# Whole fp32 query products for three of four slices, and the masks of a chunk inverse on VectorE

## The chip, the cores and the metric

The kernel runs on one core of a Trainium2 chip. The core has TensorE (PE in the profile, with its weight loads as PEld), VectorE (DVE), ScalarE (ACT), GpSimd (POOL) and the queue of SyncE (SP), and 16 DMA engines. The metric is the device time of one execution in microseconds (us); of several runs the median is given.

## The reference

One layer of a trunk over 1024 tokens of width 1024. A combined projection feeds an RWKV-7 branch (a recurrence over tokens in 8 heads of 64) and a latent attention with a block-causal mask; both are gated and added. Then comes a retrieval layer over 16,384 experts of one neuron each, then a small gated embedding and a last norm. What bears on this case:

```python
    state = state * w_t + sa[..., None] * b_t + v_t[..., None] * k_t      # RWKV-7, token by token
    ...
    def one_block(xb):                                                    # retrieval, 128 tokens
        q = (xb @ w_q).reshape(t, PEER_HEADS, 2, HALF_Q)
        s = jnp.einsum('thcd,hcnd->thcn', q, sub_keys).astype(jnp.float32)
        top_s, top_i = lax.top_k(s, PEER_TOPK)
        cand_s = (top_s[:, :, 0, :, None] + top_s[:, :, 1, None, :]).reshape(...)
        best_s, best_pos = lax.top_k(cand_s, PEER_TOPK)
        idx = jnp.take_along_axis(cand_i, best_pos, axis=-1)              # 8 heads x 16 per token
        gate = jax.nn.softmax(best_s, axis=-1)
        act = jax.nn.gelu(jnp.einsum('td,thkd->thk', xb, u_tab[idx]), approximate=False)
        return jnp.einsum('thk,thkd->td', gate * act, v_tab[idx])
```

Every token picks 128 experts. Their rows of table u (4 KB each) are multiplied with the token's activation, and their rows of table v are summed with the weights that come out.

## The kernel before, in words

The 1024 tokens are eight blocks of 128, taken two at a time as four slices (0 to 3). For each slice the kernel runs `project_rwkv` and `project_rest` (the combined projection), `rwkv` (the recurrence, in chunks of 64 tokens), `attend`, and `select`.

`rwkv` prepares chunks in `chunk_pre`: products within a chunk come to a tile `gs` (L612), and the inverse of a triangular matrix is built in six levels. At each level a mask takes one band out of `gs`: two multiplications of 128x256 into the tile `lm` (L621), which has two buffers. TensorE multiplies `lm` with the running inverse `x` (L586), and VectorE adds the product to `x` and `xt` (L642, L645). There are eight `chunk_pre`, two per slice, so 96 mask multiplications. They are made by `self.aux`, which is GpSimd while `rwkv` is written out and VectorE otherwise. GpSimd makes the token differences (L497) and three more small steps of `rwkv` too.

`select` joins the branches, projects them (L785), normalises, transposes the activation (`to_T`), and makes the queries: 16 tiles of weights `w_q`, 8 products of 128x128 by 128x256 each. Before the change every product is split: an fp32 number is written as a high part (a cast to fp32r by ScalarE, L280) and a low part (the remainder by a subtraction, L282, on GpSimd for these weights; L261 on VectorE for the activation), and high times high, high times low and low times high are summed (L292, L293, L294). The other projections take whole fp32 products (L290). The query is multiplied with the keys (L813), and VectorE finds the top 16 of each (L824 to L828). `combine` makes the 128 indices per token (up to the cast at L869).

`gather` then fetches, for each block, 128 times 128 rows of u by an indirect DMA from GpSimd's queue (L900) and has VectorE take the dot with the activation (L902). The rows land in four buffers in turn, seven from the dense product on. For blocks 0 to 4 the weighted sum over v is not gathered: `expand` spreads the weights into a dense matrix (L959, L961) which is written to memory, and `dense` multiplies it with all of v in split products (L280, L282, L996 to L998) and adds the sums (L1001). For blocks 5 to 7 the rows of v are gathered (L915) and added one by one (L917). `ple` does the last step of each block.

The order of the work is made when the kernel is built: each stage is written with a priority (a low number goes first; `gather` has a high one), and a scheduler places every instruction on its engine by these priorities and a timeline of its own. On the chip each engine takes its queue strictly in that order. So a gather on GpSimd waits behind whatever stands ahead of it in GpSimd's queue, and a dot that lacks its row holds up all that follows on VectorE.

Of the kernel before, what the change touches and what calls it, by code (L numbers as in the profile page):

```python
# [9 lines left out]
R = mybir.dt.float32r  # L10
# [141 lines left out]
class Program:  # L152
# [131 lines left out]
    def mm(self, ps, w, a, k, start=True, stop=True):  # L284

        mm = self.nc.tensor.matmul
        for i in range(k):
            first, last = start and i == 0, stop and i == k - 1
            if len(w) == 1:
                mm(ps, w[0][:, i], a[0][:, i], start=first, stop=last)  # L290
            else:
                mm(ps, w[0][:, i], a[0][:, i], start=first, stop=False)  # L292
                mm(ps, w[0][:, i], a[1][:, i], start=False, stop=False)  # L293
                mm(ps, w[1][:, i], a[0][:, i], start=False, stop=last)  # L294
# [293 lines left out]
    def chunk_pre(self, pool, psum, B):  # L588


        nc = self.nc
        t = lambda shape, tag, bufs=2: self.tile(pool, shape, F, tag, bufs)
        bank = lambda shape: self.tile(psum, shape, F, "inv", 2)
        ar, kb, v = B["ar"], B["kb"], B["v"]
        eye = self.c("eye2")
        mm = nc.tensor.matmul
        halves = (slice(0, 64), slice(64, 128))
        G, V = [], []
        for c in range(2):
            gs = t([128, 4, 2, 192], "gs", 3)  # L600
            vs = t([128, 4, 64], "vs", 3)
            ts = slice(c * 64, c * 64 + 64)
            for j in range(4):
                ps = bank([128, 448])
                for a in range(2):
                    for p in halves:
                        mm(ps[p, a * 192:a * 192 + 128], kb[p, a, j, ts], ar[p, j, c], start=True, stop=True)
                    for p in halves:
                        mm(ps[p, a * 192 + 128:a * 192 + 192], kb[p, a, j, ts], eye[p], start=True, stop=True)
                for p in halves:  # L610
                    mm(ps[p, 384:448], v[p, j, ts], eye[p], start=True, stop=True)
                nc.vector.tensor_tensor(gs[:, j], ps[:, :384].rearrange("p (a n) -> p a n", a=2),  # L612
                                        self.c("gmask")[:, None, :].to_broadcast([128, 2, 192]), op=OP.mult)
                nc.scalar.activation(vs[:, j], ps[:, 384:448], AF.Copy)
            G.append(gs)
            V.append(vs)

        def level(l):
            m = t([128, 8, 64], "lm", 2)
            for c in range(2):  # L620
                self.aux.tensor_tensor(m[:, 4 * c:4 * c + 4], G[c][:, :, 0, 0:64],  # L621
                                       self.c("lmask")[:, None, l * 64:l * 64 + 64].to_broadcast([128, 4, 64]), op=OP.mult)
            return m

        eye_b = eye[:, None, :].to_broadcast([128, 8, 64])
        lm = level(0)
        z = bank([128, 8, 64])
        self.each(z, (lambda j: lm[:, j], lambda j: eye))
        x = t([128, 8, 64], "x", 1)
        nc.vector.tensor_tensor(x, z, eye_b, op=OP.add)  # L630
        xt = t([128, 8, 64], "xt", 2)
        nc.vector.tensor_tensor(xt, lm, eye_b, op=OP.add)
        for l in range(1, 6):
            lm = level(l)
            z = bank([128, 8, 64])
            self.each(z, (lambda j: lm[:, j], lambda j: x[:, j]))
            zs = t([128, 8, 64], "zs", 1)
            nc.scalar.activation(zs, z, AF.Copy)
            if l < 5:
                d = bank([128, 8, 64])  # L640
                self.each(d, (lambda j: xt[:, j], lambda j: zs[:, j]))
                nc.vector.tensor_tensor(x, x, d, op=OP.add)  # L642
            d = bank([128, 8, 64])
            self.each(d, (lambda j: zs[:, j], lambda j: xt[:, j]))
            nc.vector.tensor_tensor(xt, xt, d, op=OP.add)  # L645
        return G, V, xt
# [106 lines left out]
    def select(self, hf, side="left"):  # L753
        nc = self.nc
        bl = SLICES[hf]
        NB, N = len(bl), len(bl) * 128
        ts = self.tile(self.kp, [128, NB, 8, 2, 16], F, "ts", 1)
        ti = self.tile(self.kp, [128, NB, 8, 2, 16], U32, "ti", 1)
        with ExitStack() as s2:
            pool = self.pool(s2, "se", side)  # L760
            psum = self.pool(s2, "sp", side, True)
            t, bank = self.makers(pool, psum)
# [4 lines left out]
            m = t([128, 8, N], "act")  # L767
            for d in range(8):
                ys = []
                for i, src in enumerate(("rw_wo", "mla_wo")):  # L770
                    w = self.weights(self.wp, self.I[src][d], 4)
# [8 lines left out]
            for k in range(8):  # L780
                w = self.tile(self.wp, [128, 8, 128], F, "w", WBUF).rearrange("p a n -> p (a n)")
# [14 lines left out]
            for b, x in zip(bl, xs):  # L796
                nc.vector.scalar_tensor_tensor(x, x, rs[:, b - bl[0]:b - bl[0] + 1], gf, op0=OP.mult, op1=OP.mult)
                nc.sync.dma_start(self.h2[b], x)
            hT = [t([128, 8, N], "act", 2, R) for _ in range(2)]
            self.to_T(bank, xs, hT)  # L800
            for i in range(16):
                raw, = self.weights(self.wp, self.I["w_q"][i], 8)
                w = [t([128, 8, 128], n, 1, R) for n in (("whi", "wlo") if i % 2 == 0 else ("x0", "x1"))]
                self.split_to(w, raw, nc.gpsimd)
                ps = bank([128, N])
                self.mm(ps, w, hT, 8)
                q = t([128, N], "gate", 4)
                nc.scalar.activation(q, ps, AF.Copy)
                keys = t([128, 128], "keys", 3)
                nc.sync.dma_start(keys, self.I["keys"][:, i])  # L810
                ps = bank([128, NB, 128], "tr", 1)
                for b in range(NB):
                    nc.tensor.matmul(ps[:, b], q[:, b * 128:b * 128 + 128], keys, start=True, stop=True)  # L813
                s = t([128, NB, 128], "s", 5)
                nc.scalar.activation(s, ps, AF.Copy)
                for b in range(NB):
                    self.top16(s[:, b], ts[:, b, i // 2, i % 2], ti[:, b, i // 2, i % 2])
# [303 lines left out]
```

## Time and profile before

| | |
|---|---|
| median of 3 runs | 3949.66 us (3947.78 to 3959.03) |
| the profiled execution | 3942.72 us, its span 3940.7 us |
| granted TensorE clock, mean | 0.880 |
| VectorE busy | 3193.8 us, 81% |
| TensorE busy | 3087.6 us, 78% |
| GpSimd busy | 2050.4 us, 52% |
| ScalarE busy | 1276.9 us, 32% |
| DMA | 1160.48 MB, mean 294 GB/s |

The page gives one execution. A row of instructions names the line, the engine, the operation, what it writes and reads, its shape and count, then its busy time and the mean of one, and behind the second bar how long the engine was idle before it and on whom it waited. The chain of waits follows the work that ended last back from the end; "issue" in it is time in which an engine waited for nothing that the profile shows. A stretch is given by its start and end in us from the span's start.

### The profile page before, as it was taken

Reading aid. Unit: us, or ns where it says so; the run is one execution under the profiler, and the core shown is the slowest. Engines: PE = TensorE matmul, PEld = TensorE weight load, DVE = VectorE, ACT = ScalarE, POOL = GpSimd, SP = SyncE. Lnnn points to the kernel's source line nnn. Section 1 sums busy time; section 2 is a strip of 40 time slices with the busy share of each in tenths; the row PEclk is TensorE's granted clock in tenths of the full one; section 3 lists DMA queues with packets and bytes.
Section 4 is the critical chain, followed back from the end, with each engine's and each line's share of the span. In section 5 each row is a group of like instructions: output and inputs, shape, how many; then the busy total and the mean of one; then the engine's idle time right before and its main releaser. Section 6 shows DMA issues by size and latency. Waiting matters only on the chain.

```text
span 3940.7 us, 62191 instructions
## 1 busy us (share of the span) xinstructions
PE 3087.6 (78%) x21999; PEld 2517.8 (64%) x21999; DVE 3193.8 (81%) x6931; ACT 1276.9 (32%) x2723; POOL 2050.4 (52%) x1638
## 2 busy tenths in 40 slices
PE   7998778678879794878866687568888889989581
PEld 7885767666668673578735567446666667767351
DVE  2532888767899685899878778998999999999997
ACT  3231222133222174222138867522221222222341
POOL 0201456645654533576454425446767776666754
PEclk9998899888989796888967788779999999999796
DMA  6236598899868998878888998799999999999986
GB/s 200 88 112 200 183 321 286 285 318 309 313 188 309 322 323 285 305 243 279 311 276 284 302 336 274 233 321 341 386 384 371 390 379 372 373 385 352 329 279 232
DMA packets 502327, 1160.48 MB, mean 294 GB/s; under 512 B 54016, under 2 KB 228352, under 8 KB 502016
## 3 DMA queue, kind: packets, MB, share of 16 engines
q0 software_dynamic: 202752, 738.29, 52.7%
q1 hardware_dynamic: 281984, 402.48, 30.3%
q10 hardware_dynamic: 17280, 15.74, 1.2%
q8 instruction: 174, 2.85, 0.3%
q14 instruction: 137, 1.12, 0.1%
HBM read 1071.38 MB, written 84.93 MB: 293 GB/s over the span
## 4 chain that ended last, share of the span: by engine, by line
DVE 23%; PE 23%; issue 20%; DMA 17%; POOL 10%; ACT 5%; SPq 2%; POOLq 0%; DVEq 0%; ACTq 0%
DVE u L902 9%; DMA u<-in_u_dram,idx 9%; PE mm L290 7%; POOL u L900 6%; POOL u L915 4%; PE mm L785 2%; DVE oa L959 2%; PE w L961 1%; PE inv L586 1%; PE acc L997 1%; DMA u<-in_v_dram,idx 1%; DMA raw<-zT 1%; PE acc L998 1%; PE mm L292 1%; SPq L964 1%
## 5 line engine op out<-in xcount | busy, mean ns | idle before, releaser
L900 POOL DMA_INDIRECT u<-in_u_dram,idx x1024 | 1230.5, 1202 | 1182.1 <-DVE dots L902 625.2
L902 DVE CUSTOM_DVE_ANT_0 u<-u,gh 128x1024 f32<-128x1024 f32 x1024 | 1320.8, 1303 | 226.8 <-DMA u<-in_u_dram,idx 210.1
L915 POOL DMA_INDIRECT u<-in_v_dram,idx x384 | 485.7, 1265 | 230.6 <-DVE x L917 104.1
L290 PE MATMUL mm<-hT,w 128*128 128x128 f32 x4608 | 568.4, 284 | 11.8 <-DMA raw<-zT 3.5
L997 PE MATMUL acc<-vlo,Whi 128*128 128x512 f32 x1280 | 521.8, 408 | 67.4 <-DVE vlo L282 66.8
L290 PEld LDWEIGHTS mm<-hT,w 128*128 128x128 f32 x4608 | 553.1, 199 | 27.6 <-ACT z L326 7.8
L998 PE MATMUL acc<-vhi,Wlo 128*128 128x512 f32 x1280 | 513.4, 401 | 0.0
L996 PE MATMUL acc<-vhi,Whi 128*128 128x512 f32 x1280 | 374.3, 402 | 101.8 <-ACT vhi L280 83.0
L996 PEld LDWEIGHTS acc<-vhi,Whi 128*128 128x128 f32 x1280 | 244.9, 193 | 176.5 <-ACT vhi L280 93.1
L997 PEld LDWEIGHTS acc<-vlo,Whi 128*128 128x128 f32 x1280 | 248.4, 194 | 147.1 <-DVE vlo L282 96.7
L917 DVE SCALAR_TENSOR_TENSOR x<-u,gate,x 128x1024 f32<-128x1024 f32 x256 | 329.2, 1286 | 6.0 <-DMA u<-in_v_dram,idx 2.1
L280 ACT ACTIVATE vhi<-vr 128x512 fp32r<-128x512 f32 x256 | 158.8, 628 | 532.2 <-DMA vr<-in_v_dram 347.6
L961 PE MATMUL w<-ob,oa 128*128 128x128 f32 x1280 | 225.3, 334 | 98.1 <-ACT ob L955 53.5
L961 PEld LDWEIGHTS w<-ob,oa 128*128 128x128 f32 x1280 | 203.6, 240 | 124.9 <-ACT ob L955 81.6
L998 PEld LDWEIGHTS acc<-vhi,Wlo 128*128 128x128 f32 x1280 | 249.1, 195 | 51.6
L959 DVE TENSOR_SCALAR oa<-cst,pt 128x128 f32<-128x128 f32 x640 | 210.7, 388 | 39.3 <-PE w L961 34.8
L954 ACT ACTIVATE ob<-cst,pt 128x128 f32<-128x128 f32 x640 | 204.3, 396 | 0.6 <-PE w L961 0.5
L282 DVE TENSOR_TENSOR vlo<-vr,vhi 128x512 fp32r<-128x512 f32 x256 | 174.7, 693 | 8.0 <-ACT vhi L280 7.9
L280 ACT ACTIVATE Whi<-wr 128x1280 fp32r<-128x1280 f32 x64 | 81.5, 1273 | 287.0 <-PE acc L997 257.6
L917 DVE SCALAR_TENSOR_TENSOR gh<-u,gate,gh 128x1024 f32<-128x1024 f32 x128 | 167.9, 1311 | 4.9 <-DMA u<-in_v_dram,idx 3.0
L290 PE MATMUL mm<-act,w 128*128 128x256 f32 x512 | 134.0, 417 | 45.2 <-DMA act<-yg 29.1
L621 POOL TENSOR_TENSOR lm<-gs,cst 128x256 f32<-128x256 f32 x96 | 100.1, 1063 | 100.9 <-DVE gs L612 56.6
(331 smaller groups left out, 5511.6 us busy)
## 6 DMA issues: line engine op xcount, KB each, us to landing
w<-in_w_in_dram SPq DMA_DIRECT2D x144, 512.0 KB
vr<-in_v_dram SPq DMA_DIRECT2D x256, 256.0 KB
W<-ws SPq DMA_DIRECT2D x40, 1024.0 KB
wr<-W SPq DMA_DIRECT2D x64, 640.0 KB
w<-in_w_q_dram SPq DMA_DIRECT2D x64, 512.0 KB
w<-in_w_out_dram SPq DMA_DIRECT2D x32, 512.0 KB
u<-in_u_dram,idx POOLq DMA_INDIRECT x1024, 6.9
x<-in_x_dram SPq DMA_DIRECT2D x16, 512.0 KB
```

The costliest lines, as they stand in the source:

```text
L280: self.nc.scalar.activation(act[0], x, AF.Copy)
L290: mm(ps, w[0][:, i], a[0][:, i], start=first, stop=last)
L900: nc.gpsimd.indirect_dma_start(out=u[:], out_offset=None, in_=self.I["u"], in_offset=bass.IndirectOffsetOnAxis(ap=idx[:, k:k + 1], axis=0))
L902: nc.vector.tensor_tensor_reduce(out=u[:], in0=u[:], in1=h[:], scale=1.0, scalar=0.0, op0=OP.mult, op1=OP.add, accum_out=dots[:, k:k + 1])
L915: nc.gpsimd.indirect_dma_start(out=v[:], out_offset=None, in_=self.I["v"], in_offset=bass.IndirectOffsetOnAxis(ap=idx[:, k:k + 1], axis=0))
L917: nc.vector.scalar_tensor_tensor(x, v, gate[:, k:k + 1], x, op0=OP.mult, op1=OP.add)
L954: nc.scalar.activation(c[:, i], self.c("iota"), AF.Abs, bias=pt[:, 1, k + i:k + i + 1])
L959: nc.vector.tensor_scalar(a, self.c("iota"), pt[:, 0, k:k + 1], pt[:, 2, k:k + 1], op0=OP.is_equal, op1=OP.mult)
L961: nc.tensor.matmul(ps[:, i], a, c[:, i], start=True, stop=True)
L996: nc.tensor.matmul(acc[b], wh, vh, start=i == 0, stop=False)
L997: nc.tensor.matmul(acc[b], wh, vl, start=False, stop=False)
L998: nc.tensor.matmul(acc[b], wl, vh, start=False, stop=i == G - 1)
```

## The change

The masks of `chunk_pre` are made by VectorE. In `select`, slice 0 keeps the split queries; slices 1 to 3 transpose the activation into one fp32 tile and multiply it with the weights as they were loaded, so that the casts, the subtractions and the split tiles of the weights, and the low part of the activation, are not made.

```diff
@@ chunk_pre, level(l)
             for c in range(2):
-                self.aux.tensor_tensor(m[:, 4 * c:4 * c + 4], G[c][:, :, 0, 0:64],
+                nc.vector.tensor_tensor(m[:, 4 * c:4 * c + 4], G[c][:, :, 0, 0:64],
                                        self.c("lmask")[:, None, l * 64:l * 64 + 64].to_broadcast([128, 4, 64]), op=OP.mult)
@@ select
-            hT = [t([128, 8, N], "act", 2, R) for _ in range(2)]
+
+            split = hf == 0
+            hT = [t([128, 8, N], "act", 2, R) for _ in range(2)] if split else [t([128, 8, N], "act")]
             self.to_T(bank, xs, hT)
             for i in range(16):
                 raw, = self.weights(self.wp, self.I["w_q"][i], 8)
-                w = [t([128, 8, 128], n, 1, R) for n in (("whi", "wlo") if i % 2 == 0 else ("x0", "x1"))]
-                self.split_to(w, raw, nc.gpsimd)
+                w = (raw,)
+                if split:
+                    w = [t([128, 8, 128], n, 1, R) for n in (("whi", "wlo") if i % 2 == 0 else ("x0", "x1"))]
+                    self.split_to(w, raw, nc.gpsimd)
                 ps = bank([128, N])
                 self.mm(ps, w, hT, 8)
```

The scheduler makes a new order from it. Lines behind L805 stand four further down in the changed kernel. GpSimd's queue among the queries of slice 1, before (`u` is a buffer of a gathered row, `wlo` and `x` are low parts of the weights), and then the same gathers in the changed order:

```order
L900 DMA u_1255_5233<-in_u_dram,idx_1010_4457 128x1024
L282 TENSOR_TENSOR wlo_9023<-w_9020,whi_9022 128x1024
L282 TENSOR_TENSOR x_1946_9073<-w_9070,x_1945_9072 128x1024
L900 DMA u_5236<-in_u_dram,idx_1010_4457 128x1024
L900 DMA u_5239<-in_u_dram,idx_1010_4457 128x1024
L900 DMA u_5242<-in_u_dram,idx_1010_4457 128x1024
L282 TENSOR_TENSOR wlo_9123<-w_9120,whi_9122 128x1024
L900 DMA u_1259_5245<-in_u_dram,idx_1010_4457 128x1024
L282 TENSOR_TENSOR x_1962_9173<-w_9170,x_1961_9172 128x1024
L900 DMA u_5248<-in_u_dram,idx_1010_4457 128x1024
```

```order
L904 DMA u_1255_5233<-in_u_dram,idx_1010_4457 128x1024
L904 DMA u_5236<-in_u_dram,idx_1010_4457 128x1024
L904 DMA u_5239<-in_u_dram,idx_1010_4457 128x1024
L904 DMA u_5242<-in_u_dram,idx_1010_4457 128x1024
L904 DMA u_1259_5245<-in_u_dram,idx_1010_4457 128x1024
L904 DMA u_5248<-in_u_dram,idx_1010_4457 128x1024
```

The splits between the gathers are gone; in the rows before, one to three gathers stood between two of them. VectorE's queue at the first levels of an inverse of slice 1, before and then changed (`krt`, `lst`, `ms` are small tiles of norms):

```order
L218 SCALAR_TENSOR_TENSOR krt_6307<-kry_6306 8x128
L630 TENSOR_TENSOR x_5969<-inv_5952,cst_60 128x512
L902 ISA u_4697,dots_4534<-u_4697,gh_4532 128x1024
L902 ISA dots_4534 128x1
L390 TENSOR_SCALAR ms_7543<-sum_7385 128x256
L902 ISA u_1077_4700,dots_4534<-u_1077_4700,gh_4532 128x1024
L902 ISA dots_4534 128x1
```

```order
L218 SCALAR_TENSOR_TENSOR krt_6307<-kry_6306 8x128
L630 TENSOR_TENSOR x_5969<-inv_5952,cst_60 128x512
L906 ISA u_1077_4700,dots_4534<-u_1077_4700,gh_4532 128x1024
L906 ISA dots_4534 128x1
L621 TENSOR_TENSOR lm_6031<-gs_5841,cst_60 128x256
L621 TENSOR_TENSOR lm_6031<-gs_5895,cst_60 128x256
L906 ISA u_4703,dots_4534<-u_4703,gh_4532 128x1024
L906 ISA dots_4534 128x1
```

Each level's two masks now stand among the dots, here behind one that reads a gathered row. The last place is VectorE's queue at the end of the dense product: its last sums into the blocks' rows (`x` from `acc`), before and then changed.

```order
L917 SCALAR_TENSOR_TENSOR x_6608_30642<-u_30983,gate_4131_20116,x_6608_30642 128x1024
L1001 TENSOR_TENSOR x_5354_24164<-x_5354_24164,acc_6450_30076 128x512
L1001 TENSOR_TENSOR x_5355_24166<-x_5355_24166,acc_6451_30077 128x512
L1001 TENSOR_TENSOR x_5356_24168<-x_5356_24168,acc_6452_30078 128x512
L1001 TENSOR_TENSOR x_5357_24170<-x_5357_24170,acc_6453_30079 128x512
L917 SCALAR_TENSOR_TENSOR x_6608_30642<-u_30986,gate_4131_20116,x_6608_30642 128x1024
L1001 TENSOR_TENSOR x_5358_24172<-x_5358_24172,acc_6454_30080 128x512
```

```order
L921 SCALAR_TENSOR_TENSOR gh_30041<-u_6672_30142,gate_4047_19230,gh_30041 128x1024
L1005 TENSOR_TENSOR x_5255_23177<-x_5255_23177,acc_6351_29089 128x512
L1005 TENSOR_TENSOR x_5256_23179<-x_5256_23179,acc_6352_29090 128x512
L921 SCALAR_TENSOR_TENSOR gh_30041<-u_30145,gate_4047_19230,gh_30041 128x1024
L1005 TENSOR_TENSOR x_5257_23181<-x_5257_23181,acc_6353_29091 128x512
L1005 TENSOR_TENSOR x_5258_23183<-x_5258_23183,acc_6354_29092 128x512
L1005 TENSOR_TENSOR x_5259_23185<-x_5259_23185,acc_6355_29093 128x512
```

Before, the additions of v rows have come to block 6 (`x_6608`) when the dense product ends: 243 additions stand ahead. Changed, they have come to block 7, whose rows are summed in `gh`: 291 stand ahead. Likewise 731 dots stand ahead of the dense product's first low part of v (`vlo`, L282) before, and 768, all of blocks 0 to 5, in the changed order.

## The prediction

> **What bounds the kernel now.** I read the page's busy shares first, then the engines by stretches of the run.
>
> ```profile
> PE 3087.6 (78%) x21999; PEld 2517.8 (64%) x21999; DVE 3193.8 (81%) x6931; ACT 1276.9 (32%) x2723; POOL 2050.4 (52%) x1638
> 0.00:480.00 480.00, 410.05 (x4111) 356.81 (x4112) 200.84 (x733) 134.27 (x298) 79.64 (x67) 0.94 0.48 151
> 480.00:1000.00 520.00, 403.03 (x4104) 345.74 (x4102) 399.66 (x813) 134.29 (x289) 291.76 (x254) 0.89 0.90 309
> 1000.00:1170.00 170.00, 136.28 (x1367) 110.79 (x1368) 155.57 (x414) 37.67 (x77) 107.19 (x78) 0.92 0.77 252
> 1170.00:1660.00 490.00, 392.22 (x3013) 317.12 (x3015) 370.87 (x950) 187.91 (x447) 214.30 (x193) 0.85 0.89 302
> 1660.00:1800.00 140.00, 110.54 (x1216) 100.64 (x1217) 136.57 (x352) 35.88 (x71) 102.41 (x70) 0.83 0.76 247
> 1800.00:2380.00 580.00, 432.36 (x3028) 336.41 (x3026) 477.30 (x1267) 303.89 (x745) 276.42 (x230) 0.81 0.90 300
> 2380.00:2577.00 197.00, 115.72 (x774) 109.59 (x772) 191.23 (x644) 116.91 (x293) 92.44 (x67) 0.77 0.81 265
> 2577.00:3650.00 1073.00, 939.36 (x3835) 733.85 (x3836) 1011.08 (x1408) 242.54 (x333) 711.23 (x541) 0.96 0.98 368
> ```
>
> The columns are the stretch, PE, its weight loads, VectorE (DVE), ScalarE, GpSimd (POOL), the granted clock, the share of the DMA engines and GB/s. The short stretches at 1000, 1660 and 2380 us hold the queries of slices 1, 2 and 3: VectorE is busy 92%, 98% and 97% there, and DMA is at its lowest. Between them DMA stands near 0.90 and VectorE at 76 to 82%. From 2577 us (the dense product with table v) DMA is full. The chain of waits of two stretches agrees:
>
> ```profile
> by line: DVE u L902 50.5%; DVE ti L825 5.3%; DVE s L826 4.9%; DVE ti L828 4.6%; DVE ts L824 3.9%; DMA u<-in_u_dram,idx 3.6%; DVE ts L827 3.6%; DVE x L797 2.4%; issue 2.1%; DVE H L669 1.8%; DVE x L642 1.7%; DVE gs L612 1.7%; DVE xt L645 1.7%
> by line: DMA u<-in_u_dram,idx 15.8%; issue 15.5%; DVE u L902 7.6%; POOL u L900 6.7%; PE mm L290 6.1%; SPq L964 4.3%; PE mm L785 4.3%; DMA W<-ws 3.2%; PE w L961 3.1%; DMA w<-in_mla_wo_dram 2.7%; ACT ob L954 2.5%; DMA keys<-in_keys_dram 1.9%;
> ```
>
> The first is 1660 to 1800 us, a query stretch: VectorE's dots (L902) and top-16 sets it. The second is 1170 to 1660 us: mostly the loop of gathers. What sets that loop:
>
> ```profile
> L900 POOL DMA_INDIRECT u<-in_u_dram,idx x1024 | 1230.5, 1202 | 1182.1 <-DVE dots L902 625.2 <-DVE oa L959 119.2 <-issue 111.5
> L902 DVE DVE_READ_ACCUMULATOR2_ANT dots<- 128x1 f32 x1024 | 80.5, 79 | 0.0
> u<-in_u_dram,idx POOLq DMA_INDIRECT x1024, 6.9
> DVE u L902 <- DMA u<-in_u_dram,idx: 210.1, 202, 4.3
> POOL u L900 <- DVE dots L902: 625.2, 342, 15.2
> 480.00:1000.00 520.00, 229.07 (x200) 0.89 0.90 309
> 1170.00:1660.00 490.00, 189.74 (x172) 0.85 0.89 302
> 1800.00:2380.00 580.00, 256.07 (x215) 0.81 0.90 300
> ```
>
> The last three rows count the gathers on GpSimd: 587 in 1590 us, 2.70 us each. The least that four row buffers allow is one turn through GpSimd (1.2 us, L900), landing (6.9) and dot (1.22, a row below, and 0.08 for its read-out), 9.4 us, over four: 2.35 us.
>
> **The change part by part.** *The splits of slices 1 to 3 leave GpSimd.* Their price is seen in VectorE's dots; the rows are groups of VectorE by stretch (560:960, 1040:1165, 1700:1810, 2380:2510 with two rows, 2070:2370 with two rows).
>
> ```profile
> L902 DVE CUSTOM_DVE_ANT_0 u<-u,gh 128x1024 f32<-128x1024 f32 x156 | 200.7, 1294 | 67.6 <-DMA u<-in_u_dram,idx 63.3 <-DMA gh<-h 3.9
> ...
> L902 DVE CUSTOM_DVE_ANT_0 u<-u,gh 128x1024 f32<-128x1024 f32 x38 | 73.7, 1947 | 4.6 <-DMA u<-in_u_dram,idx 4.6
> ...
> L902 DVE CUSTOM_DVE_ANT_0 u<-u,gh 128x1024 f32<-128x1024 f32 x35 | 70.1, 2006 | 3.4 <-DMA u<-in_u_dram,idx 3.4
> ...
> L959 DVE TENSOR_SCALAR oa<-cst,pt 128x128 f32<-128x128 f32 x115 | 57.4, 549 | 4.2 <-PE w L961 3.7 <-ACT pt L945 0.5
> L902 DVE CUSTOM_DVE_ANT_0 u<-u,gh 128x1024 f32<-128x1024 f32 x28 | 40.4, 1448 | 0.2 <-DMA u<-in_u_dram,idx 0.2
> ...
> L902 DVE CUSTOM_DVE_ANT_0 u<-u,gh 128x1024 f32<-128x1024 f32 x104 | 125.3, 1217 | 25.4 <-DMA u<-in_u_dram,idx 21.4 <-DMA gh<-h 3.8
> L959 DVE TENSOR_SCALAR oa<-cst,pt 128x128 f32<-128x128 f32 x352 | 102.4, 350 | 30.9 <-PE w L961 27.3 <-ACT pt L945 1.6
> ```
>
> In 2070:2370 GpSimd does no arithmetic and a dot takes 1217 ns; while the splits run it takes 1947 and 2006. So 38 x 0.730 + 35 x 0.789 + 28 x 0.231 = 27.7 + 27.6 + 6.5 us, and 115 x 0.199 = 22.9 us at L959: 84.7 us of VectorE's time are its waiting for GpSimd's splits (with ten masks that fall in these stretches). It lies where VectorE is 92 to 98% busy, so I count it whole. Bounds: 0, if the dots then wait for their gathers instead, and 84.7.
>
> *The masks move from GpSimd to VectorE*, and eight subtractions per slice of the transposed act (L261) fall away.
>
> ```profile
> L621 POOL TENSOR_TENSOR lm<-gs,cst 128x256 f32<-128x256 f32 x96 | 100.1, 1063 | 100.9 <-DVE gs L612 56.6 <-PE inv L586 41.6 <-DVE xt L632 2.1
> L282 POOL TENSOR_TENSOR wlo<-w,whi 128x1024 fp32r<-128x1024 f32 x32 | 78.0, 2438 | 101.4 <-ACT whi L280 101.0
> L282 POOL TENSOR_TENSOR x<-w,x 128x1024 fp32r<-128x1024 f32 x32 | 76.9, 2404 | 19.1 <-ACT x L280 17.8
> L778 DVE TENSOR_TENSOR act<-gate,gate x32: 393/422/1247, 317.1 to 2333.5; 128x256 f32<-128x256 f32 x32
> L261 DVE TENSOR_TENSOR act<-mm,act 128x256 fp32r<-128x256 f32 x32 | 12.2, 414 | 3.2 <-ACT act L255 3.2
> ```
>
> A product of two 128x256 tiles takes VectorE 0.42 us (L778, the middle figure; no row has the mask's strided reading, so 0.40 to 0.55). Of 96 masks 24 are slice 0's, before 480 us, where VectorE is busy 201 us of 480: nothing (10 us if that cover is gone). The other 72 add 30.2 us. L261 gives back 24 x 0.414 = 9.9 us. The dots that collided with masks outside the query stretches: in 560:960 they cost 156 x 0.077 = 12 us, part of it by arithmetic that stays on GpSimd (L497, L548); 0 to 12, I take 8. VectorE's sum is -84.7 - 8 + 30.2 - 9.9 = **-72.4 us**.
>
> [...]
>
> *GpSimd's queue.* It loses 48 splits (116 us) and 72 masks (77 us), and gathers no longer stand behind a mask that waits for gs or a split that waits for ScalarE. What that speeds beyond the dots lies between nothing (GpSimd mostly waits for VectorE, the 625.2 us above) and the 210.1 us that dots wait for gathers. Nearest is the first: I take **-15 us**.
>
> *The products.* The records of slice 1's split product, and of a whole fp32 product of the same width:
>
> ```profile
> 1078.73 0.28 PE L292 MATMUL mm<-act,whi 128*128 128x256 f32 x1
> ...
> 1080.29 0.28 PE L293 MATMUL mm<-act,whi 128*128 128x256 f32 x1
> 2293.90 3.62 PE L290 MATMUL mm<-act,w 128*128 128x256 f32 x16
> ```
>
> From the first to the second row are 13 steps in 1.56 us: 0.12 us each, 384 per slice, 46 us. The fp32 product leaves two records, and the sixteen of the last row (eight products) start 0.216 us apart (3.62 less 0.38 for one record, over 15): 0.43 us each, 128 per slice, 55 us. So PE gets 9 us slower per slice, not faster. The stretches of the queries are 140 to 197 us long and set by VectorE; that hides it, and if the cover is gone it costs 27 us. I take **+3**. ScalarE loses the 48 casts of those splits at 32% load: nothing. The raw weights stay in their four buffers until PE has read them; 16 loads in 140 us leave 8.8 us for each, and I see no cost. No byte of DMA changes.
>
> The sum is -72.4 - 15 + 3 = -84 us: 3942.7 - 84 = 3858 us for a profiled execution. The median of the runs stood 6.9 us above the profiled one, so **3865**.
>
> *Where it should show.* The changed order puts 768 dots ahead of the dense product's first vlo (731 before) and 291 additions of v rows ahead of its last sum (243). An addition is 1.286 us:
>
> ```profile
> L917 DVE SCALAR_TENSOR_TENSOR x<-u,gate,x 128x1024 f32<-128x1024 f32 x256 | 329.2, 1286 | 6.0 <-DMA u<-in_v_dram,idx 2.1
> ```
>
> So 48 fewer stand behind the dense product: -62 us. The dense product itself carries 256 + 291 gathers where it carried 293 + 243; 11 more of 524 KB at 368 GB/s are +16. The rest, -38 us, is the time up to its start, with 37 more dots (48 us) done in it.
>
> **Rivals.** *The gather loop takes the relief back.* The 37 additional dots cost the loop's 2.70 us each instead of VectorE's 1.3: +100 against -84 ahead of the dense product, then -46: 3942.7 - 30 = 3913, at the runs' level 3920. For it: the second chain above. Against it: in 1040:1165 a dot came every 3.3 us and without the stalls still every 2.56, above the loop's 2.35; in 1700:1810 just at it (2.35).
>
> *Slower: the masks and whole products lengthen the chain of the inverse.* In slices 1 to 3 there are 36 levels; each now has two masks (0.84 us) in VectorE's queue, behind dots that wait for gathers (1.04 us a wait, 210.1 over 202). Queued behind them are the additions to x and xt, for which PE waits:
>
> ```profile
> L586 PE MATMUL inv<-x,lm 64*64 64x64 f32 x1280 | 58.8, 244 | 53.7 <-DVE x L642 45.7 <-DVE x L630 6.1 <-DVE nrst L218 1.9
> ```
>
> If that chain sets the pace, 36 x 1.88 = 68 us and PE's 27 come on, the dots' relief turns to idle time, and -46 remains: +49, 3999. It decides once a mask pair comes later than the level's x. Against it: the masks read only gs, so all but the two buffers' turn is free to run ahead, and the 45.7 us are few.
>
> *GpSimd's free queue speeds every gather.* If the 587 gathers outside the query stretches came every 2.5 us instead of 2.70, that is 117 us more: 3749. Against it DMA's 0.90 there.
>
> That the change does not do what it says is out: after slice 0 the changed order has no split of queries and no mask on GpSimd.
>
> **How the numbers follow.** The forecast has 0.60, its own range 3825 to 3900; the loop 0.20; the slower chain 0.11; the faster gathers 0.09. 3790 to 3935 leaves out most of the last two. About 0.3% is what a measurement of this kernel can tell. Within it lie some of the loop's and of the slower case's share, 0.07 together; slower keeps 0.10; faster 0.83.
>
> **What would show it.** Dots in the query stretches at about 1.22 us and L959 at 0.35; VectorE under 90% busy there or the stretches some 25 us shorter; the dense product starting near 2540 us with 768 dots done; the last v additions some 50 us shorter; L621 on VectorE near 0.42 us. It would be wrong if dots wait for gathers in the query stretches (the loop), or if PE's wait before inv names L621 (the slower chain).

## The result, and the profile after

The changed kernel takes **3856.72 us** (median of 4 runs, 3850.12 to 3864.38) where the kernel before takes 3948.72 (3944.41 to 3959.03): a ratio of 0.9757 by the record's estimate from the single runs, with an interval of 0.9735 to 0.978 (the two medians alone give 0.977). That is 92 us less; 3865 was predicted. Three executions of those reported below, one each of the kernel before, the first run and the seventh, came at a granted clock of 0.78, 0.68 and 0.63 and took 4057, 4342 and 4635 us; the ratios leave them out. The profiled execution took 3855.49 us, its span 3853.7 at a granted clock of 0.888.

The engines' busy times on the page of the changed kernel, and then the same stretches as before (stretch, PE, its weight loads, VectorE, ScalarE, GpSimd, granted clock, DMA share, GB/s):

```profile
PE 3104.5 (81%) x21615; PEld 2506.3 (65%) x21615; DVE 3110.8 (81%) x7003; ACT 1243.0 (32%) x2682; POOL 1856.3 (48%) x1494
```

```profile
480.00:1000.00 520.00, 425.95 (x4177) 349.81 (x4177) 402.90 (x831) 135.09 (x290) 262.41 (x222) 0.90 0.91 312
1000.00:1170.00 170.00, 139.65 (x1337) 126.58 (x1338) 154.08 (x563) 33.72 (x80) 67.82 (x60) 0.91 0.82 288
...
1660.00:1800.00 140.00, 118.73 (x1035) 104.91 (x1036) 128.39 (x480) 21.46 (x58) 70.68 (x59) 0.85 0.84 294
...
2380.00:2577.00 197.00, 114.96 (x552) 99.44 (x551) 182.09 (x688) 105.37 (x262) 75.29 (x63) 0.72 0.88 295
```

VectorE is busy 91%, 92% and 92% in the stretches of the queries (92%, 98% and 97% before), and DMA moves more there: 0.82, 0.84 and 0.88 where it was 0.77, 0.76 and 0.81. These stretches are fixed in time, and the queries in them now begin 16 to 62 us earlier (rows of the top-8 search, further down); between the first and the last of these searches VectorE was 100% busy before and is now 98%, 95% and 96%. The dots, by groups of VectorE in these stretches (1030:1140, 1680:1785, and two rows of 2360:2480), have the length that they had before only in a stretch where GpSimd does no arithmetic (1217 ns, 2070 to 2370 us):

```profile
L906 DVE CUSTOM_DVE_ANT_0 u<-u,gh 128x1024 f32<-128x1024 f32 x41 | 49.8, 1219 | 8.9 <-DMA u<-in_u_dram,idx 8.7
...
L906 DVE CUSTOM_DVE_ANT_0 u<-u,gh 128x1024 f32<-128x1024 f32 x44 | 53.3, 1216 | 6.7 <-DMA u<-in_u_dram,idx 6.6
...
L906 DVE CUSTOM_DVE_ANT_0 u<-u,gh 128x1024 f32<-128x1024 f32 x42 | 50.9, 1216 | 0.4 <-DMA u<-in_u_dram,idx 0.4
L963 DVE TENSOR_SCALAR oa<-cst,pt 128x128 f32<-128x128 f32 x121 | 36.4, 357 | 0.5 <-PE w L965 0.5
```

They took 1947, 2006 and 1448 ns, and the one-hot row 549. What it comes to over the whole run stands in the groups of VectorE before and after:

```profile
L902 DVE CUSTOM_DVE_ANT_0 u<-u,gh 128x1024 f32<-128x1024 f32 x1024 | 1320.8, 1303 | 226.8 <-DMA u<-in_u_dram,idx 210.1 <-DMA gh<-h 14.1
L959 DVE TENSOR_SCALAR oa<-cst,pt 128x128 f32<-128x128 f32 x640 | 210.7, 388 | 39.3 <-PE w L961 34.8 <-ACT pt L945 2.1
```

```profile
L906 DVE CUSTOM_DVE_ANT_0 u<-u,gh 128x1024 f32<-128x1024 f32 x1024 | 1249.9, 1233 | 220.0 <-DMA u<-in_u_dram,idx 201.8 <-issue 10.6 <-DMA gh<-h 3.9
L963 DVE TENSOR_SCALAR oa<-cst,pt 128x128 f32<-128x128 f32 x640 | 190.2, 354 | 47.4 <-PE w L965 44.0 <-PE mm L290 1.9
L621 DVE TENSOR_TENSOR lm<-gs,cst 128x256 f32<-128x256 f32 x96 | 40.3, 460 | 8.1 <-PE inv L586 7.9
```

Dots and one-hots need 70.9 + 20.5 = 91.4 us less; the masks bring 40.3 us (0.42 us each by the total, in which records that overlap count once; the row's mean of single records is 460 ns); the dots' wait for their rows has hardly moved (210.1 to 201.8). The first row of `vlo` and the last of the dense sums place the gain, by the tiles' rows of VectorE (shortest, median, longest ns; first and last start), before and after:

```profile
L282 DVE TENSOR_TENSOR vlo<-vr,vhi x256: 668/683/1834, 2588.1 to 3644.3; 128x512 fp32r<-128x512 f32 x128
...
L1001 DVE TENSOR_TENSOR x<-x,acc x160: 670/679/689, 2630.1 to 3653.1; 128x512 f32<-128x512 f32 x160
```

```profile
L282 DVE TENSOR_TENSOR vlo<-vr,vhi x256: 666/685/2153, 2552.8 to 3627.1; 128x512 fp32r<-128x512 f32 x128
...
L1005 DVE TENSOR_TENSOR x<-x,acc x160: 673/680/690, 2601.5 to 3633.7; 128x512 f32<-128x512 f32 x160
```

The dense product starts 35 us earlier, with 37 more dots done; from its start to its last sum it takes 16 us longer (1065 to 1081); and what follows the last sum, to the end of the span, falls from 287 to 219 us, with 48 fewer additions left to do.

### The profile page after: what moved, and what is told of

It reads as the page before. It is cut to its first block, busy times and chain, and to the rows that moved or that the text cites. A ratio compares the mean times of both kernels' runs of the same rounds, so it can differ in the third digit from the quotient of the medians.

```text
span 3853.7 us, 61140 instructions
## 1 busy us (share of the span) xinstructions
PE 3104.5 (81%) x21615; PEld 2506.3 (65%) x21615; DVE 3110.8 (81%) x7003; ACT 1243.0 (32%) x2682; POOL 1856.3 (48%) x1494
## 4 chain that ended last, share of the span: by engine, by line
PE 25%; DVE 23%; issue 20%; DMA 17%; POOL 9%; ACT 4%; SPq 1%; POOLq 0%; DVEq 0%; ACTq 0%; another core or an unknown queue 0%
DMA u<-in_u_dram,idx 9%; PE mm L290 9%; DVE u L906 8%; POOL u L904 6%; POOL u L919 3%; PE mm L785 2%; PE acc L1001 2%; DVE oa L963 2%; PE acc L1002 1%; DVE gh L921 1%; PE acc L1000 1%; DMA gate<-zT 1%; DMA raw<-zT 1%; PE w L965 1%; DVE x L921 1%
## 5 line engine op out<-in xcount | busy, mean ns | idle before, releaser
L904 POOL DMA_INDIRECT u<-in_u_dram,idx x1024 | 1248.3, 1219 | 1284.3 <-DVE dots L906 681.8
L906 DVE CUSTOM_DVE_ANT_0 u<-u,gh 128x1024 f32<-128x1024 f32 x1024 | 1249.9, 1233 | 220.0 <-DMA u<-in_u_dram,idx 201.8
L290 PEld LDWEIGHTS mm<-hT,w 128*128 128x128 f32 x4608 | 544.7, 197 | 27.7 <-issue 8.8
L290 PE MATMUL mm<-act,w 128*128 128x256 f32 x1280 | 313.6, 399 | 33.5 <-DVE gate L776 14.6
L290 PEld LDWEIGHTS mm<-act,w 128*128 128x128 f32 x1280 | 247.8, 200 | 73.8 <-issue 16.9
L963 DVE TENSOR_SCALAR oa<-cst,pt 128x128 f32<-128x128 f32 x640 | 190.2, 354 | 47.4 <-PE w L965 44.0
L282 DVE TENSOR_TENSOR vlo<-vr,vhi 128x512 fp32r<-128x512 f32 x256 | 175.3, 697 | 5.1 <-ACT vhi L280 5.1
```

What stands on the lines that cost most here:

```text
L904: nc.gpsimd.indirect_dma_start(out=u[:], out_offset=None, in_=self.I["u"], in_offset=bass.IndirectOffsetOnAxis(ap=idx[:, k:k + 1], axis=0))
L906: nc.vector.tensor_tensor_reduce(out=u[:], in0=u[:], in1=h[:], scale=1.0, scalar=0.0, op0=OP.mult, op1=OP.add, accum_out=dots[:, k:k + 1])
L963: nc.vector.tensor_scalar(a, self.c("iota"), pt[:, 0, k:k + 1], pt[:, 2, k:k + 1], op0=OP.is_equal, op1=OP.mult)
```

## The experiments

The theory: an instruction of GpSimd that reads holds up VectorE's dots, and VectorE's time so lost is what the change gives back. That it is the reading is my assumption. Against the theory stand three others: it is GpSimd's queue (its being occupied, whatever the instruction does), it is the products that wait for GpSimd, or it is the masks. Differences of a few us are not read below: the six kernels whose GpSimd makes no subtraction in the queries of slices 1 to 3 (the changed one, and the second, fourth, fifth, sixth and eighth run here) lie between 3840.7 and 3858.7, each with an order of its own from the scheduler. I take 10 us either way as the worth of the order alone; it is the spread of six kernels and not a bound. The runs were made in rounds, with the kernel before in each, and its median moved between 3942.9 and 3952.2, so a difference of two medians from different rounds carries some 9 us more.

### The two halves of the change

The first run puts only the masks on VectorE, in the kernel before; the second keeps the whole products and gives the masks back to GpSimd.

```diff
 first run, against the kernel before
-                self.aux.tensor_tensor(m[:, 4 * c:4 * c + 4], G[c][:, :, 0, 0:64],
+                nc.vector.tensor_tensor(m[:, 4 * c:4 * c + 4], G[c][:, :, 0, 0:64],
 second run, against the changed kernel
-                nc.vector.tensor_tensor(m[:, 4 * c:4 * c + 4], G[c][:, :, 0, 0:64],
+                self.aux.tensor_tensor(m[:, 4 * c:4 * c + 4], G[c][:, :, 0, 0:64],
```

> The kernel before with one part of the change alone: the masks of the chunk inverse on VectorE; the queries stay split, with their low parts on GpSimd. My theory (the gain is VectorE's waiting for GpSimd's splits, which stay here): 72 masks add 30 us to VectorE among the gathers, some 8 to 19 us of collisions with masks go, so no gain: 3945 to 3970 us against 3949. Rival (GpSimd's queue is what counts, and the gathers behind waiting masks were the loss): 3890 to 3920 us.

> The other part alone: whole fp32 queries in slices 1 to 3, masks still on GpSimd. My theory: nearly all of the gain, since the 85 us that VectorE waits for the splits go: 3850 to 3875 us, dots of the query stretches near 1.22 us. Rival (each part gives about half): 3895 to 3915 us.

Masks alone: 3934.57 us, ratio 0.9949 (0.9929 to 0.9968), about 17 us less. It lies between the two expectations and meets neither. Whole products alone: 3858.65 us, ratio 0.9766 (0.9736 to 0.9796), the whole gain. The second meets what the theory expected. So the masks are worth 17 us in the kernel before, by a way that no run here shows (VectorE is busy 16 us more there), and nothing beside the whole products. The change's effect is that of the splits.

### What a GpSimd instruction must do to cost time

Three kernels add to the changed one 48 GpSimd instructions in the queries of slices 1 to 3, whose result is used by nothing that counts. In all three ScalarE writes one column into the same tile behind each product, so that its buffer turns with the products, and waits for the added instruction there (149 to 186 us in all).

```diff
                 if split:
                     w = [t([128, 8, 128], n, 1, R) for n in (("whi", "wlo") if i % 2 == 0 else ("x0", "x1"))]
                     self.split_to(w, raw, nc.gpsimd)
+                if not split:
+                    dummy = t([128, 8, 128], "x0", 1)                # third run
+                    nc.gpsimd.tensor_tensor(dummy, raw, raw, op=OP.subtract)
+                    dummy = t([128, 8, 384], "x0", 1)                # fourth run, in its place
+                    nc.gpsimd.memset(dummy, 0.0)
+                    dummy = t([128, 8, 128], "x0", 1)                # tenth run, in its place
+                    nc.gpsimd.tensor_tensor(dummy, raw, hT[0][:, :, 0:128], op=OP.subtract)
                 ps = bank([128, N])
                 self.mm(ps, w, hT, 8)
+                if not split:
+                    nc.scalar.activation(dummy[:, 0, 0:1], ps[:, 0:1], AF.Copy)
```

> The changed kernel with 48 subtractions put back on GpSimd: in slices 1 to 3 each loaded tile of query weights is subtracted from itself into a tile that nobody uses (same shape as the low part, about 2.4 us each); products stay whole. My theory (VectorE's dots wait while GpSimd reads the on-chip memory): dots of the query stretches back at 1.9 to 2.0 us and 60 to 90 us lost, 3915 to 3950 us. Rival (it was TensorE's split products, the casts or the two-stage wait for them that cost the time, not GpSimd's arithmetic): 3855 to 3870 us.

> As the run with the 48 subtractions, but GpSimd only writes: 48 fills with zero of 128x3072 at the same places, meant to hold GpSimd's queue for about as long without reading. My theory: the dots stay at 1.22 us, the queue has room, 3855 to 3880 us. Rival (the gathers behind the arithmetic in GpSimd's queue are what is late): like the run with subtractions, 3900 us or more.

> The changed kernel with 48 subtractions on GpSimd as before, but of two different tiles (weights and activation), so that one lasts some 2.4 us and not the 1.97 us of the earlier run; the result is used by nobody. If the cost goes with the time that VectorE's dots and one-hot tiles lose: about 80 us lost there and 3885 to 3905 us. If whole products simply bear it better, 3870 to 3885 us; if it is as in the split kernel, 3920 us or more.

The groups of the added instruction, the dots and the one-hots: in the tenth run (a subtraction of two tiles), and in the fourth (a fill):

```profile
L911 DVE CUSTOM_DVE_ANT_0 u<-u,gh 128x1024 f32<-128x1024 f32 x1024 | 1297.8, 1279 | 199.9 <-DMA u<-in_u_dram,idx 193.2 <-DMA gh<-h 2.7 <-DVE vlo L282 0.4
...
L968 DVE TENSOR_SCALAR oa<-cst,pt 128x128 f32<-128x128 f32 x640 | 215.0, 393 | 40.7 <-PE w L970 36.5 <-ACT pt L954 2.6
...
L811 POOL TENSOR_TENSOR x<-w,act 128x1024 f32<-128x1024 f32 x48 | 114.7, 2389 | 7.9 <-ACT ob L964 6.5 <-ACT x L815 0.3
```

```profile
L911 DVE CUSTOM_DVE_ANT_0 u<-u,gh 128x1024 f32<-128x1024 f32 x1024 | 1247.6, 1230 | 210.0 <-DMA u<-in_u_dram,idx 191.6 <-issue 9.9 <-DMA gh<-h 5.7
...
L968 DVE TENSOR_SCALAR oa<-cst,pt 128x128 f32<-128x128 f32 x640 | 217.0, 439 | 33.0 <-PE w L970 31.7
...
L811 POOL MEMSET x<- 128x3072 f32 x48 | 128.5, 2678 | 3.2 <-ACT x L815 2.0 <-PE mm L252 0.9 <-issue 0.3
```

The tenth run takes 3903.21 us, ratio 0.9904 (0.9885 to 0.9922): 46 us over the changed kernel, within what the theory expected of it. Its dots and one-hots need (1297.8 - 1249.9) + (215.0 - 190.2) = 72.7 us more. The fourth run occupies GpSimd longer (128.5 us against 114.7) in the same places, and takes 3845.85 us, ratio 0.9748 (0.9702 to 0.9794): no more than the changed kernel. So GpSimd's queue being occupied costs nothing; a subtraction, which reads, does. (A fill also computes nothing; an instruction that reads without computing was not run.) Single rows show it: in the tenth run a dot that meets a subtraction ends 1.1 us behind the subtraction's end, about a whole dot later, and in the fourth one that meets a fill takes its usual time (tenth run first, then fourth; start and length in us):

```profile
1069.50 2.35 POOL L811 TENSOR_TENSOR x<-w,act 128x1024 f32<-128x1024 f32 x1
1069.17 3.77 DVE L911 CUSTOM_DVE_ANT_0 u<-u,gh 128x1024 f32<-128x1024 f32 x1
```

```profile
1071.02 2.67 POOL L811 MEMSET x<- 128x3072 f32 x1
1071.23 1.20 DVE L911 CUSTOM_DVE_ANT_0 u<-u,gh 128x1024 f32<-128x1024 f32 x1
```

In the query stretches of slices 1 and 2 (1040 to 1140, and 1695 to 1790 us in the tenth run, 1680 to 1780 in the fourth), 28 of the 32 dots that overlap a subtraction end 1.07 to 1.21 us behind its end; the other four had begun before it and were through within 0.5 us of its start. All 41 dots that overlap a fill take 1.20 to 1.23 us. The fills do lengthen the one-hots, by 26.8 us in all (217.0 against 190.2), as much as the subtractions do, and the kernel is no slower for it. Between the fourth and the tenth run only the dots differ: 50.2 us of them, for 57 us of the time. The third run, which reads one tile twice, has shorter subtractions and lies between:

```profile
L911 DVE CUSTOM_DVE_ANT_0 u<-u,gh 128x1024 f32<-128x1024 f32 x1024 | 1292.9, 1275 | 197.9 <-DMA u<-in_u_dram,idx 176.5 <-issue 11.2 <-DMA gh<-h 6.8
L968 DVE TENSOR_SCALAR oa<-cst,pt 128x128 f32<-128x128 f32 x640 | 206.5, 377 | 45.2 <-PE w L970 41.7 <-PE mm L785 1.3 <-ACT ws L971 0.8
...
L811 POOL TENSOR_TENSOR x<-w 128x1024 f32<-128x1024 f32 x48 | 94.5, 1968 | 8.9 <-ACT x L815 4.3 <-DMA w<-in_w_q_dram 2.9 <-PE mm L252 0.8
```

It takes 3881.59 us, ratio 0.9826 (0.9795 to 0.9858), between its two expectations and in neither: 25 us for 43.0 + 16.3 = 59.3 us of VectorE's time.

### The split, and the products that wait for it

Three kernels start from the kernel before with the masks on VectorE, and change what GpSimd does for slices 1 to 3 while PE still makes 24 products of fp32r a tile.

```diff
                 w = [t([128, 8, 128], n, 1, R) for n in (("whi", "wlo") if i % 2 == 0 else ("x0", "x1"))]
 fifth run
-                self.split_to(w, raw, nc.gpsimd)
+                if hf == 0:
+                    self.split_to(w, raw, nc.gpsimd)
+                else:
+                    w = (w[0], w[0])
+                    self.split_to(w[:1], raw)
 sixth run
-                self.split_to(w, raw, nc.gpsimd)
+                if hf == 0:
+                    self.split_to(w, raw, nc.gpsimd)
+                else:
+                    self.split_to(w[:1], raw)
+                    for _ in range(3):
+                        nc.gpsimd.memset(w[1].bitcast(F), 0.0)
 ninth run
                 self.split_to(w, raw, nc.gpsimd)
+                if hf > 0:
+                    w = (w[0], w[0])
```

> Masks on VectorE; in slices 1 to 3 the queries are three products per tile as before, but the low part of the weights is left out and the high part stands in its place (so the queries' third term is other than in the reference). TensorE and ScalarE do what they did before the change, GpSimd does nothing for the queries. If GpSimd's work is the whole cause, this is as fast as the changed kernel or some us faster (TensorE has 27 us less): 3830 to 3860 us. If the split itself (three products, casts, their buffers) cost the time: 3900 us or more.

> As the run before, but the products wait again for GpSimd: the low part is filled with zeros by three writes of 128x1024 (about 2.7 us together, the time of a subtraction), which read nothing; the low part's value is left out. The subtraction's wait and its place in GpSimd's queue are kept, its reading is not. If the reading (collisions with VectorE's dots) is what costs: 3840 to 3870 us, dots at 1.22 us. If the products' and gathers' wait in GpSimd's queue costs: 3900 to 3935 us, like the run with masks alone. The 48 subtractions in the earlier run cost only 25 us, so I now expect something between: 3880 to 3910.

> Masks on VectorE; split products with the high part in place of the low one (as in the run without GpSimd), and GpSimd makes the 48 subtractions of the low parts again, into tiles that nobody reads. Reading by GpSimd is back, the products' wait for it is not. If the collisions alone cost the time: 3915 to 3940 us, like masks alone (3935). If a collision costs only where a product waits for the subtraction: 3860 to 3890 us, like the whole products with 48 idle subtractions (3882).

In the fifth run GpSimd does nothing for these queries; in the sixth the products wait for GpSimd's fills; in the ninth GpSimd makes every subtraction and no product reads what comes of it. With the first run, where products wait for the subtraction, they make a square:

| | no product reads what GpSimd makes | products wait for what GpSimd makes |
|---|---|---|
| GpSimd subtracts nothing | fifth: 3850.43 us, 0.9752 (0.9725 to 0.9779) | sixth, fills: 3840.71 us, 0.9734 (0.9689 to 0.9779) |
| GpSimd subtracts | ninth: 3902.34 us, 0.9907 (0.9886 to 0.9929) | first: 3934.57 us, 0.9949 (0.9929 to 0.9968) |

The ratios are to the kernel before. The sixth run came out faster than the 3880 to 3910 us that I had come to expect, where the reading alone as the cause had 3840 to 3870; the ninth lies between its two expectations. Groups of VectorE and GpSimd in the fifth, the ninth and the sixth run:

```profile
L906 DVE CUSTOM_DVE_ANT_0 u<-u,gh 128x1024 f32<-128x1024 f32 x1024 | 1246.5, 1228 | 208.8 <-DMA u<-in_u_dram,idx 195.4 <-DMA gh<-h 10.5
L963 DVE TENSOR_SCALAR oa<-cst,pt 128x128 f32<-128x128 f32 x640 | 186.8, 354 | 41.5 <-PE w L965 35.6 <-ACT pt L949 3.9
```

```profile
L904 DVE CUSTOM_DVE_ANT_0 u<-u,gh 128x1024 f32<-128x1024 f32 x1024 | 1302.0, 1283 | 197.1 <-DMA u<-in_u_dram,idx 177.0 <-DMA gh<-h 18.1
L961 DVE TENSOR_SCALAR oa<-cst,pt 128x128 f32<-128x128 f32 x640 | 218.5, 398 | 35.0 <-PE w L963 33.6
```

```profile
L907 DVE CUSTOM_DVE_ANT_0 u<-u,gh 128x1024 f32<-128x1024 f32 x1024 | 1245.1, 1230 | 215.4 <-DMA u<-in_u_dram,idx 202.5 <-DMA gh<-h 10.4
L964 DVE TENSOR_SCALAR oa<-cst,pt 128x128 f32<-128x128 f32 x640 | 216.3, 432 | 33.0 <-PE w L966 31.9
...
L809 POOL MEMSET wlo<- 128x1024 f32 x72 | 70.0, 972 | 8.5 <-PE mm L294 5.8 <-ACT t L514 2.1
L809 POOL MEMSET x<- 128x1024 f32 x72 | 69.7, 968 | 0.9 <-PE mm L294 0.3
```

Three things follow. The split products cost no more than the whole ones (3850.4 beside 3856.7). Waiting for GpSimd costs nothing by itself: three fills, 2.9 us together, are longer than a subtraction of 2.44, and the sixth run is among the fastest. Subtracting costs 52 us with nobody reading the result (fifth to ninth, for (1302.0 - 1246.5) + (218.5 - 186.8) = 87.2 us of VectorE's time), and 94 us with products waiting (sixth to first). The ninth run isn't free of waiting, though: the next cast into a tile waits for the subtraction that still reads it, and PE waits 13.6 us for such casts. The first and the sixth run have no such wait.

```profile
ACT x L280 <- POOL x L282: 30.8, 10, 5.1
ACT whi L280 <- POOL wlo L282: 27.5, 10, 5.1
```

The step from the ninth to the first run, when the products wait for the subtraction itself, is 32 us by the medians and some 17 by the ratios, whose intervals touch at 0.9929. What in that wait costs them is not settled, nor is the order ruled out: a subtraction also has to wait for ScalarE's cast, which a fill does not, and PE's own waits for the low parts, `wlo` and `x`, are no longer in the first run than in the sixth (15.1 us, and 21.6, by the rows of the third product, L294).

### Twice as many masks

```diff
-                nc.vector.tensor_tensor(m[:, 4 * c:4 * c + 4], G[c][:, :, 0, 0:64],
+                for _ in range(2):
+                  nc.vector.tensor_tensor(m[:, 4 * c:4 * c + 4], G[c][:, :, 0, 0:64],
```

> The changed kernel with every mask made twice on VectorE: 96 more instructions of about 0.45 us, 32 us among the gathers. It prices a microsecond of VectorE's queue ahead of the dense product. If VectorE sets the pace: 20 to 40 us slower than the changed kernel, 3877 to 3897 us. If the added work falls into idle time: 3855 to 3865 us. If the masks stand on the chain of the inverse, as the slower rival has it: over 3900 us.

```profile
L622 DVE TENSOR_TENSOR lm<-gs,cst 128x256 f32<-128x256 f32 x192 | 76.2, 435 | 12.2 <-PE inv L586 12.1
```

VectorE's masks take 36 us more (76.2 against 40.3), and the kernel 3843.99 us, ratio 0.9739 (0.9712 to 0.9767): not slower than with one set, and below all three expectations. This work falls into time in which VectorE would have waited: its idle time in the span goes from 743 to 701 us.

### Five buffers for the gathered rows

If the turn of four row buffers held the gain back, a fifth should free it.

```diff
-ROWS = (4, 7)
+ROWS = (5, 7)
```

> The changed kernel with five instead of four row buffers until the dense product (seven from there on, as before). The least spacing of gathers falls from 2.35 to 1.88 us. If VectorE's queue sets the pace ahead of the dense product: 3835 to 3860 us. If the gather loop does (the rival that takes the relief back): 3760 to 3820 us, with the spacing outside the query stretches under 2.5 us.

> The kernel with five row buffers once more, for a profile at an undisturbed clock, since the first run of it came out slower than the changed kernel (3897 us) against both expectations. If more gathers in flight hold up the loads of the main chain: transfers of weights take longer, the gathers outside the query stretches come nearer than in the changed kernel, and VectorE or TensorE wait more for other DMAs. If it is the order alone: the same spacing and the same waits, and the time lies in another place.

It takes 3897.49 us in the one run and 3891.52 in the other, ratios 0.9862 (0.9826 to 0.9898) and 0.9853 (0.9769 to 0.9936): some 35 to 40 us *slower* than the changed kernel, against both expectations of the first of them. The rows are of the second, which has two executions. Its stretches from 480 and 1000 us, its longest wait of gathers for indices, and the projection of slice 1 (L785, first to last start), the last then for the changed kernel:

```profile
480.00:1000.00 520.00, 384.97 (x3789) 324.31 (x3787) 398.25 (x838) 118.82 (x256) 312.23 (x243) 0.83 0.93 326
1000.00:1170.00 170.00, 153.23 (x1176) 116.84 (x1176) 118.50 (x436) 36.04 (x85) 35.03 (x31) 0.98 0.62 207
...
POOL u L904 <- DVE idx L873: 265.7, 4, 95.8
...
L785 PE MATMUL mm<-w,act x48: 592/592/697, 1037.9 to 1073.1; 128*128 128x512 f32 x48
```

```profile
L785 PE MATMUL mm<-w,act x48: 592/592/697, 962.5 to 995.5; 128*128 128x512 f32 x48
```

Gathers do come faster up to 1000 us (DMA 0.93, 326 GB/s). But slice 1's projection starts 75 us later, PE having done 41 us less by then at a granted clock of 0.83 (0.90); then block 1's rows are all fetched before there are new indices, gathers wait 266 us for them in four places (77 us in the changed kernel), and DMA stands at 0.62 from 1000 to 1170 us. That the faster gathers delayed the projection, rather than the order that came with the fifth buffer or the lower clock, is my reading and wasn't tested alone.

### GpSimd left with gathers only

The last one moves all arithmetic of GpSimd except slice 0's query splits to VectorE: the token differences, the three small steps of `rwkv`, and `ple`'s splits.

```diff
-                self.split_to([x[:, i] for x in w], raw, nc.gpsimd if i % 2 else nc.vector)
+                self.split_to([x[:, i] for x in w], raw, nc.vector)
...
-                self.aux = nc.gpsimd if f == self.rwkv else nc.vector
+                self.aux = nc.vector
```

> The changed kernel with all arithmetic of GpSimd but slice 0's splits moved to VectorE: the token differences and small steps of the recurrence, and half of the splits of the last stage's weights. About 31 and 7 us of VectorE's time come on, and the collisions that are left (some 40 us in the changed kernel's trace) go. If collisions cost more than VectorE's own time, as the runs with doubled masks and with fills say: 3830 to 3850 us. If VectorE's time counts the same: 3850 to 3860 us.

```profile
PE 3095.3 (81%) x21615; PEld 2502.7 (66%) x21615; DVE 3097.5 (81%) x7069; ACT 1236.7 (32%) x2677; POOL 1792.8 (47%) x1428
...
L906 DVE CUSTOM_DVE_ANT_0 u<-u,gh 128x1024 f32<-128x1024 f32 x1024 | 1234.8, 1217 | 216.8 <-DMA u<-in_u_dram,idx 204.3 <-DMA gh<-h 9.6
```

It takes **3800.28 us** (3788.22 to 3808.68), ratio 0.9631 (0.9607 to 0.9656): 56 us faster than the changed kernel, and better than either theory expected. All 1024 dots now average 1217 ns. VectorE does 66 more instructions and is busy 13 us less than in the changed kernel. Where the rest of the 56 us comes from isn't shown. A candidate is that GpSimd's differences stood behind gathers in its queue, on the way to each recurrence: in the changed kernel VectorE waits 52 us for them (L499 for L497, in ten waits), and here these waits are gone. No run isolates it.

## Why the prediction came out right, point by point

The time (92 us less by the medians, 87 by the profiled executions, 84 predicted) was right, and so was the cause. The terms were not all of the right size, and their errors went both ways; that the sum came within 3 to 8 us is in part luck.

- **The splits' hold on VectorE (-84.7, and -8 for masks).** As VectorE's time it was right: 92.7 predicted, 91.4 measured. That "I count it whole" was the step that failed. In the ninth run 87 us of such time cost 52, in the tenth 73 cost 46, in the third 59 cost 25: 0.4 to 0.65 us of the kernel's time for one lost. At the ninth's ratio, 91 us are worth about 55. The runs place the failure with the one-hots (22.9 of the 84.7): in the fourth and the sixth run the fills lengthen them by 26.8 and 29.5 us (against the changed kernel and the fifth run), and these kernels are among the fastest. Over the dots alone the ninth run has 52 us for 55.5, the tenth 46 for 47.9, the third 25 for 43.0, so counting the dots' part nearly whole may have been right. A late dot also frees its row buffer late for the next gather (gathers wait 681.8 us for dots in the changed kernel), which a one-hot doesn't; that this makes the difference was not tested. That subtractions hold up the dots and fills don't is measured: over all 1024 the dots average 1279 ns with the subtractions of the tenth run, 1230 with the fills of the fourth and 1233 in the changed kernel. That the subtraction's reading does it was my assumption; no run shows it apart from the computing.
- **The masks on VectorE (+30.2, L261 -9.9).** Their duration was right (0.42 us, 40.3 in all), their price wasn't: the second run and the doubled masks put it at nothing that can be told from the order's spread, and in the kernel before the masks alone gained 17 us. For L261 no run shows a price; its rows went from 12.2 us to 3.2.
- **GpSimd's queue (-15).** Mis-sized, and named for the wrong thing. Occupying the queue costs nothing (fourth and sixth run, 3845.85 and 3840.71 us beside 3856.72). What else the splits held up were the products that waited for them, worth 17 to 32 us in the square, inside the bounds of 0 to 210 and up to twice the value taken.
- **The products (+3).** Held: the fifth run, with split products, is 6 us faster than the changed kernel, which is within the spread. That fits the work that was to hide PE's longer products.

With the measured sizes, about -55 (up to -71 if the dots count whole), 0, -17 to -32 and 0 to +6 make -66 to -103. The 92 us lie within it; the split among the terms is no finer than that.

*Where it should show.* -38, +16 and -62 were predicted; -35, +16 and -68 came. This part rests on the order, and the sixth run shows that the division is no test of the terms: its first `vlo` starts at 2492.7 us and its whole gain lies ahead of the dense product:

```profile
L282 DVE TENSOR_TENSOR vlo<-vr,vhi x256: 674/683/761, 2492.7 to 3543.6; 128x512 fp32r<-128x512 f32 x128
```

*The signs named.* Dots at 1.22 us and the one-hots at 0.35 came. VectorE isn't under 90% in the query stretches (91, 92 and 92%, and 95 to 98% within the queries themselves). They are shorter by 24, 27 and 7 us where some 25 was said, by the first and last start of the first top-8 search of each query, before and after, in slices 1, 2 and 3:

```profile
L824 DVE MAX8 ts<-s x32: 265/270/286, 1072.0 to 1164.5; 128x8 f32<-128x128 f32 x32
...
L824 DVE MAX8 ts<-s x32: 265/272/288, 1708.3 to 1806.0; 128x8 f32<-128x128 f32 x32
...
L824 DVE MAX8 ts<-s x32: 268/271/285, 2420.8 to 2541.0; 128x8 f32<-128x128 f32 x32
```

```profile
L828 DVE MAX8 ts<-s x32: 274/284/299, 1045.3 to 1113.4; 128x8 f32<-128x128 f32 x32
...
L828 DVE MAX8 ts<-s x32: 269/282/297, 1692.0 to 1762.8; 128x8 f32<-128x128 f32 x32
...
L828 DVE MAX8 ts<-s x32: 269/281/296, 2359.2 to 2472.9; 128x8 f32<-128x128 f32 x32
```

*The rivals.* The gather loop took nothing back: in the query stretches dots wait 0.4 to 8.9 us for their rows. A fifth buffer, meant to loosen that loop, made the kernel slower; as the order changed with it, that says little of the loop itself. The slower chain is out: PE's wait before `inv` has fallen from 53.7 us to 26.0, nothing in it names the masks, and doubling them did no harm:

```profile
L586 PE MATMUL inv<-x,lm 64*64 64x64 f32 x1280 | 53.8, 234 | 26.0 <-DVE x L642 23.8 <-issue 1.6 <-DVE x L630 0.4
```

Nor did the free queue speed every gather: GpSimd's rows have 597 of them in the three stretches outside the queries where 587 stood, 2.66 us each instead of 2.70.

## What to carry to other kernels

Compare one instruction's mean duration between stretches before looking at what waits for what: here VectorE was 92% and 98% busy in two stretches where more than a third of a dot's time (1947 and 2006 ns, against 1217 where GpSimd did no arithmetic) was lost while GpSimd's subtractions ran, and busy time does not show it. Don't price the lost time by one rate: here the dots' part came out between half and whole, the one-hots' and the added masks' at nothing. Ask separately who waits for the instruction that holds the other up (17 to 32 us here). Work added to an engine with waits between its instructions can be free even at 81% busy, as 36 us of masks were here; test it by doubling it.

## What the runs showed of the hardware that was not expected

- The GpSimd fills left the dots alone (1230 ns in the fourth and the sixth run, 1233 in the changed kernel), but lengthened VectorE's one-hot comparison: 354 ns on average in the changed kernel, 439 and 432 with the fills of the fourth and sixth run, 393 and 398 with the subtractions of the tenth and ninth. In busy time, where records that overlap count once, fills and subtractions cost it alike: 217.0 and 216.3 us, and 215.0 and 218.5. Why the one-hots and not the dots is not shown.
- A GpSimd subtraction of a tile from itself took 1968 ns, of two tiles 2389 (128x1024, fp32; third and tenth run), and it cost 25 us where the other cost 46. The lost VectorE time (59 against 73 us) does not explain all of that.
